# A Conformer convolution module with MLP: the convolution of two spilled blocks in taps of 1024 tokens instead of 512, and three PSUM banks for products instead of five

## The chip, the cores and the metric

One NeuronCore of a Trainium2 chip runs the kernel; all work is float32 in and out. The metric is the device time of one execution in microseconds (us). Before the change it is 1913.57 us, the median of 3 runs (1912.0 to 1917.03).

## What is computed

x has 2048 tokens of 1024 channels. One layer: the Conformer convolution module on the RMS-normed input, added to x, then a squared-ReLU MLP with a hidden width of 4096, added again.

```python
def conformer_conv(x, w_in, b_in, conv_w, conv_b, ln_g, ln_b, w_out, b_out):
    a, g = jnp.split(x @ w_in + b_in, 2, axis=-1)
    h = a * jax.nn.sigmoid(g)                                  # GLU
    h = depthwise_causal_conv(h, conv_w) + conv_b              # 31 taps, each channel by itself
    h = jax.nn.silu(layer_norm(h, ln_g, ln_b))
    return h @ w_out + b_out

x = x + conformer_conv(rms_norm(x, mix_norm), ...)
x = x + square(relu(rms_norm(x, mlp_norm) @ w1)) @ w2
```

## The kernel before

Channels lie on the 128 partitions, tokens along the free axis. The 1024 channels are KD = 8 channel tiles j, the 2048 tokens NB = 4 blocks b of T = 512. Each fp32 operand is kept as two fp32r halves, a rounded one and the rest (`halves`, L92 on ScalarE and L93 on VectorE or GpSimd), and a product takes three matmuls for each 128 rows of its inner dimension (`mm`, matmul at L163): 24 matmuls for an inner dimension of 1024, 12 for the 512 of one hidden group in `mlp_down`.

**First phase** (up to `front.close()`):

- GLU: for each channel tile j and block b, `glu_mm` takes two PSUM banks with `bank()`, pa for the value and pg for the gate, and fills pa, then pg. `glu` empties them. In block 0 the gate is read on VectorE at L328 (times the RMS factor, into `sg`), then the value at L331 (into `ar`), and h is formed at L335. In the other blocks ScalarE reads the gate (sigmoid, L326), and VectorE the value (L335). Blocks 0 and 1 are kept in SBUF, blocks 2 and 3 go to DRAM (`spill`, one tile for each j and block, with a halo of 30 tokens in front).
- `conv`: 31 taps on VectorE. The first (L349) writes an accumulator `cacc` in PSUM, the other 30 (L352) each read the shifted h and the accumulator and write the accumulator; the last writes over h. Blocks 0 and 1 read h, blocks 2 and 3 a tile `hc` of 128x542 that was loaded from `spill`.
- Stats and LayerNorm: `Stats.add` sums the channel tiles (L215), TensorE forms the mean (L226), the variance for each token (L235) and spreads the inverse root (L262), all on one bank of its own (`lps`). For blocks 2 and 3, `ln_spilled` does the taps, the mean, the subtraction (L387), the squares and the last step (`normalised`, L357), and each of its three steps writes `conv_out` in DRAM and loads it again for the next.
- `project` (evicted at L404), its later norm (L412) and split (L93); `mlp_up` and `mlp_down` for eight hidden groups g of 512 channels, `mlp_down` evicted at L440, all for blocks 0 and 1. `mlp_up` ends with two steps on ScalarE (L427 and the square) and the split of hid on VectorE (L93).

**Second phase**: the projection and MLP of blocks 2 and 3 with other pools (L631 and on), which take over the PSUM of the first.

Every accumulator, product and statistic lies in PSUM's 8 banks of 128x512 fp32: in the first phase `lps` takes 1, the pool `psp` of products 5, the pool `psc` of convolution accumulators 2. `bank()` hands out the banks of `psp` as they come free: a product can start when the one that last had its bank has been emptied.

The program is written in the order above; a scheduler merges it into one order for each engine by data, buffers and priority. The taps have no near deadline and fill VectorE's order wherever nothing else is ready. Each engine works its own order strictly in turn; an eviction that stands behind taps waits for them. All loads of the tiles named here go through the DMA queue of SP.

Of the kernel before, what the change touches and what calls it, by code (L numbers as in the profile page):

```python
# [59 lines left out]
def conformer_mlp(ctx: ExitStack, tc, xT, w_in, w_out, w1, w2, vecs, conv_w, outT):  # L60
# [8 lines left out]
    psp = front.enter_context(tc.tile_pool(name="psp", bufs=5, space=PSUM))  # L69
    psc = front.enter_context(tc.tile_pool(name="psc", bufs=2, space=PSUM))  # L70
# [229 lines left out]
    spill = [[dram.tile([P, HALO + T], F32, name=f"spill{j}_{i}") for i in range(2)] for j in range(KD)]  # L300
    conv_out = [[dram.tile([P, T], F32, name=f"conv{j}_{i}") for i in range(2)] for j in range(KD)]
# [20 lines left out]
    def glu(j, b, pa, pg, rs=None):  # L322
# [13 lines left out]
        if b == 0:  # L336
            nc.gpsimd.memset(h[:, :HALO], 0.0)
        else:
            nc.scalar.copy(h[:, :HALO], tails[j])
        if b < NB - 1:  # L340
            nc.scalar.copy(tails[j], h[:, T : T + HALO])
        if not keep:
            nc.sync.dma_start(spill[j][b - 2], h[:, : HALO + T])
# [3 lines left out]
    def conv(j, h):  # L347
        acc = psc.tile([P, T], F32, name="cacc", tag="cacc")
        nc.vector.tensor_scalar(acc, h[:, 0:T], cw[:, j, 0:1], v(V_CB + j), ALU.mult, ALU.add)  # L349
        for k in range(1, TAPS):  # L350
            out = acc if k < TAPS - 1 else h[:, HALO : HALO + T]
            nc.vector.scalar_tensor_tensor(out, h[:, k : k + T], cw[:, j, k : k + 1], acc, ALU.mult, ALU.add)  # L352
        return h[:, HALO : HALO + T]
# [23 lines left out]
    def ln_spilled(i):  # L377

        st = Stats(True)
        for j in range(KD):  # L380
            c = conv(j, stream("hc", spill[j][i], HT, "hc"))
            st.add(j, c)
            nc.sync.dma_start(conv_out[j][i], c)
        mu = st.mean()
        for j in range(KD):
            c = stream("c", conv_out[j][i], tag="hc")
            nc.vector.tensor_sub(c, c, mu)  # L387
            st.add_square(j, c, nc.vector)
            nc.sync.dma_start(conv_out[j][i], c)
        rs = st.rstd()  # L390
        for j in range(KD):
            s = normalised(j, stream("xc", conv_out[j][i], tag="hc"), rs)
            nc.sync.dma_start(conv_out[j][i], s)
# [138 lines left out]
    for i in range(2):  # L532
        ln_spilled(i)
# [175 lines left out]
    def second_input(i):  # L709
        ss = Split()  # L710
        for j in range(KD):
            ss.add(loaded(conv_out[j][i], "s"))
# [349 lines left out]
```

## Time and profile before

| | |
|---|---|
| runs | 1917.03, 1912.0, 1913.57 us; median 1913.57 |
| profiled execution | 1916.64 us, of it a span of 1914.9 us |
| mean granted clock of TensorE | 0.994 |
| busy | TensorE 98%, its weight loads 80%, VectorE 82%, ScalarE 40%, GpSimd 22% |
| taps of blocks 2 and 3 | 16 L349, 464 L352 into `cacc`, 16 L352 into `hc` |
| moved by DMA | 257.96 MB, mean 135 GB/s |

How to read it. Times of the trace are from the start of the span. A timeline row gives start, length, engine, line, operation, output<-inputs, the number of like instructions in sequence, and in brackets the idle time of that engine just before, with what ended it. A group row gives busy time and the mean length of one instruction, then the idle time of the engine before these. Matmuls are pipelined, so the length of one is longer than the distance from one to the next. Line numbers are those of the kernel before; in the changed kernel, lines from L349 on stand 1 lower in `conv` (L350, L353) and 8 lower from `project` on (L412 is L420, L440 is L448).

### The profile page before, as it was taken

The numbers are of one execution on the slowest core, as the hardware profiler recorded it, in microseconds if no ns is written. First come the engines' busy times: TensorE is split into PE (matmuls) and PEld (weight loads), VectorE is DVE, ScalarE is ACT, GpSimd is POOL, SyncE is SP. The second block draws the span as 40 slices with busy tenths as digits, with TensorE's granted clock in tenths as the row PEclk, the third lists the DMA queues.
The fourth block names the chain that finished last, engine by engine and source line by source line (L and its number), as shares of the span: only waits on it lengthen the run. The fifth ranks groups of instructions, "written<-read, shape, count | busy, mean of one in ns | idle before, by whom it ended". The sixth has DMA issues, their size and how long they took to land.

```text
span 1914.9 us, 22348 instructions
## 1 busy us (share of the span) xinstructions
PE 1872.0 (98%) x8192; PEld 1533.9 (80%) x8192; DVE 1576.6 (82%) x2216; ACT 766.1 (40%) x1100; POOL 417.2 (22%) x303
## 2 busy tenths in 40 slices
PE   7999999999989999999999999999999999999999
PEld 5888888888867877877888877778888887888887
DVE  7999999999999999869999974468765648869684
ACT  5323226243353333343323142436544556435431
POOL 2255522544434651000000001122100000010000
PEclk9999999999999999999999999999999999999999
DMA  5123221422223433373212146866534326677652
GB/s 207 66 89 98 98 83 62 143 101 91 97 72 106 148 110 112 113 251 110 89 63 71 66 144 217 266 219 209 203 138 163 123 104 218 180 186 186 143 143 99
DMA packets 114733, 257.96 MB, mean 135 GB/s; under 512 B 10560, under 2 KB 37312, under 8 KB 114624
## 3 DMA queue, kind: packets, MB, share of 16 engines
q1 hardware_dynamic: 104128, 219.84, 34.7%
q0 software_dynamic: 10496, 36.71, 7.4%
q8 instruction: 64, 1.05, 0.2%
q14 instruction: 45, 0.37, 0.1%
HBM read 194.39 MB, written 62.11 MB: 134 GB/s over the span
## 4 chain that ended last, share of the span: by engine, by line
PE 32%; issue 16%; DVE 4%; DMA 4%; POOL 2%; ACT 1%; SPq 0%; POOLq 0%; DVEq 0%; ACTq 0%
PE ps L163 17%; PE px L631 7%; PE pz L631 3%; PE px L163 3%; PE py L631 2%; DVE act L573 1%; POOL hid L746 1%; DMA s<-conv 1%; DVE w L605 1%; DMA conv<-s 1%; DMA rawq<-in_w 1%; DVE ld L866 1%; DMA conv<-c 0%; DMA c<-conv 0%; POOL p L796 0%
## 5 line engine op out<-in xcount | busy, mean ns | idle before, releaser
L163 PE MATMUL ps<-act,w 128*128 128x512 f32 x2880 | 666.1, 391 | 11.6 <-ACT w L92 9.2
L163 PEld LDWEIGHTS ps<-act,w 128*128 128x128 f32 x2880 | 541.3, 188 | 128.2 <-ACT w L92 9.2
L163 PE MATMUL ps<-hid,w 128*128 128x512 f32 x1920 | 445.4, 391 | 6.6 <-DVE hid L93 5.5
L163 PEld LDWEIGHTS ps<-hid,w 128*128 128x128 f32 x1920 | 360.0, 188 | 86.9 <-DVE hid L93 8.0
L631 PE MATMUL px<-act,w 128*128 128x512 f32 x1536 | 363.0, 391 | 3.4 <-DVE act L573 1.4
L631 PEld LDWEIGHTS px<-act,w 128*128 128x128 f32 x1536 | 289.0, 188 | 65.6 <-DVE act L573 2.1
L352 DVE SCALAR_TENSOR_TENSOR cacc<-hc,cw,cacc 128x512 f32<-128x512 f32 x464 | 324.8, 750 | 1.4
L352 DVE SCALAR_TENSOR_TENSOR cacc<-h,cw,cacc 128x512 f32<-128x512 f32 x464 | 317.0, 750 | 0.0
L93 POOL TENSOR_TENSOR w<-raw,w 128x1024 fp32r<-128x1024 f32 x90 | 217.2, 2413 | 287.6 <-ACT w L92 285.1
L92 ACT CAST w<-raw 128x1024 fp32r<-128x1024 f32 (+1 forms) x150 | 155.0, 1035 | 288.1 <-PE ps L163 283.5
L604 ACT CAST w<-rawq 128x1024 fp32r<-128x1024 f32 (+1 forms) x120 | 105.6, 880 | 209.2 <-PE px L631 103.8
L631 PE MATMUL pz<-act,w 128*128 128x512 f32 x768 | 182.5, 389 | 1.3 <-DVE p L729 1.3
L631 PEld LDWEIGHTS pz<-act,w 128*128 128x128 f32 x768 | 143.9, 188 | 32.3 <-ACT w L604 1.2
L605 DVE TENSOR_TENSOR w<-rawq,w 128x1024 fp32r<-128x1024 f32 (+1 forms) x120 | 121.6, 1019 | 45.8 <-ACT w L604 45.7
L440 DVE TENSOR_TENSOR h<-h,ps 128x512 f32<-128x512 f32 x128 | 86.9, 684 | 28.3 <-PE ps L163 26.6
L427 ACT ACTIVATE relu<-ps 128x512 f32<-128x512 f32 x64 | 38.2, 597 | 161.0 <-PE ps L163 160.7
L163 PE MATMUL px<-act,w 128*128 128x512 f32 x384 | 93.5, 404 | 5.2 <-DVE act L93 2.5
L163 PEld LDWEIGHTS px<-act,w 128*128 128x128 f32 x384 | 74.5, 195 | 23.3 <-DVE act L93 3.9
L631 PE MATMUL py<-act,w 128*128 128x512 f32 x384 | 90.9, 389 | 0.0
L631 PEld LDWEIGHTS py<-act,w 128*128 128x128 f32 x384 | 72.1, 188 | 15.0
L93 DVE TENSOR_TENSOR w<-raw,w 128x1024 fp32r<-128x1024 f32 (+1 forms) x60 | 71.0, 1187 | 15.4 <-ACT w L92 15.3
L215 POOL TENSOR_TENSOR acc<-acc,hc 128x512 f32<-128x512 f32 x12 | 14.0, 1165 | 252.1 <-DVE hc L352 202.0
(139 smaller groups left out, 1557.7 us busy)
## 6 DMA issues: line engine op xcount, KB each, us to landing
raw<-in_w SPq DMA_DIRECT2D x104, 512.0 KB, 3.9
rawq<-in_w SPq DMA_DIRECT2D x76, 512.0 KB, 3.9
xt<-in_xT SPq DMA_DIRECT2D x64, 256.0 KB, 3.7
ld<-hid SPq DMA_DIRECT2D x32, 512.0 KB, 5.6
raw<-in_w_in SPq DMA_DIRECT2D x30, 512.0 KB, 3.3
raw<-in_w_out SPq DMA_DIRECT2D x16, 512.0 KB, 3.4
rawq<-in_w_out SPq DMA_DIRECT2D x16, 512.0 KB, 5.8
x<-x SPq DMA_DIRECT2D x32, 256.0 KB, 3.9
```

The lines of the kernel that those rows point to most:

```text
L92: nc.scalar.copy(hl[:, 0, :], src)
L93: eng.tensor_sub(hl[:, 1, :], src, hl[:, 0, :].bitcast(F32))
L163: nc.tensor.matmul(ps, lhsT=w(k, a), rhs=x[:, b, :], start=k == 0 and i == 0, stop=k == len(xs) - 1 and i == 2,)
L352: nc.vector.scalar_tensor_tensor(out, h[:, k : k + T], cw[:, j, k : k + 1], acc, ALU.mult, ALU.add)
L427: nc.scalar.activation(r, ps, AF.Relu)
L440: nc.vector.tensor_add(x2[i][m], x2[i][m], ps)
L573: nc.vector.tensor_sub(t[:, 1], src, t[:, 0].bitcast(F32))
L604: nc.scalar.copy(hl[:, 0, :n], src)
L605: eng.tensor_sub(hl[:, 1, :n], src, hl[:, 0, :n].bitcast(F32))
L631: nc.tensor.matmul(ps, lhsT=hl[:, a, off : off + P], rhs=x[:, b, :], start=first and k == 0 and i == 0, stop=k == n - 1 and i == 2, skip_g ...
L746: nc.gpsimd.dma_start(hid_d[self.q // 4][:, self.q % 4, i : i + t.shape[1], :], t)
L866: nc.vector.tensor_sub(r[t], r[a], r[b])
```

## The change

The convolution of blocks 2 and 3 is done for both at once. `spill[j]` holds both blocks in a row (the halo, block 2, block 3), so block 3 needs no halo copies of its own. `conv_spilled` loads 128x1054 into a new tile `hw`, runs 31 taps of 128x1024 over an accumulator of 1024 fp32 (two banks, one buffer), adds each half to its own `Stats`, and writes both halves with one transfer. Then `ln_spilled` runs for block 2 and for block 3. The 496 taps of 512 become 248 of 1024; 16 loads of spill become 8, and 16 first writes of `conv_out` 8. PSUM: `lps` 1, `cacc512` 2, `cacc1024` 2, so `psp` has 3 banks left.

```diff
-    psp = front.enter_context(tc.tile_pool(name="psp", bufs=5, space=PSUM))
-    psc = front.enter_context(tc.tile_pool(name="psc", bufs=2, space=PSUM))
+    psp = front.enter_context(tc.tile_pool(name="psp", bufs=3, space=PSUM))
+    psc = front.enter_context(tc.tile_pool(name="psc", bufs=1, space=PSUM))
...
-    spill = [[dram.tile([P, HALO + T], F32, name=f"spill{j}_{i}") for i in range(2)] for j in range(KD)]
-    conv_out = [[dram.tile([P, T], F32, name=f"conv{j}_{i}") for i in range(2)] for j in range(KD)]
+    spill = [dram.tile([P, HALO + 2 * T], F32, name=f"spill{j}") for j in range(KD)]
+    conv_out = [dram.tile([P, 2, T], F32, name=f"conv{j}") for j in range(KD)]
...
         if not keep:
-            nc.sync.dma_start(spill[j][b - 2], h[:, : HALO + T])
+            at, end = (0, HALO + T) if b == 2 else (HALO + T, HALO + 2 * T)
+            nc.sync.dma_start(spill[j][:, at:end], h[:, HALO + T - (end - at) : HALO + T])
...
-    def conv(j, h):
-        acc = psc.tile([P, T], F32, name="cacc", tag="cacc")
+    def conv(j, h, n=T):
+        acc = psc.tile([P, n], F32, name="cacc", tag=f"cacc{n}", bufs=2 if n == T else 1)
...
-            out = acc if k < TAPS - 1 else h[:, HALO : HALO + T]
-            nc.vector.scalar_tensor_tensor(out, h[:, k : k + T], cw[:, j, k : k + 1], acc, ALU.mult, ALU.add)
+            out = acc if k < TAPS - 1 else h[:, HALO : HALO + n]
+            nc.vector.scalar_tensor_tensor(out, h[:, k : k + n], cw[:, j, k : k + 1], acc, ALU.mult, ALU.add)
...
-    def ln_spilled(i):
-
-        st = Stats(True)
+    def conv_spilled():
+
+        sts = [Stats(True) for _ in range(2)]
         for j in range(KD):
-            c = conv(j, stream("hc", spill[j][i], HT, "hc"))
-            st.add(j, c)
-            nc.sync.dma_start(conv_out[j][i], c)
+            h = sb.tile([P, HALO + 2 * T], F32, name="hw", tag="hw", bufs=2)
+            nc.sync.dma_start(h, spill[j])
+            c = conv(j, h, 2 * T)
+            for i in range(2):
+                sts[i].add(j, c[:, i * T : (i + 1) * T])
+            nc.sync.dma_start(conv_out[j], c.rearrange("p (i c) -> p i c", i=2))
+        return sts
+
+    def ln_spilled(i, st):
+
         mu = st.mean()
...
-    for i in range(2):
-        ln_spilled(i)
+    for i, st in enumerate(conv_spilled()):
+        ln_spilled(i, st)
     front.close()
```

What the scheduler makes of it, at three places.

TensorE, the pair of products of channel tile 0 of block 1 (`ps_551` is its value and `ps_552` its gate before; `ps_535` and `ps_536` after; the matmuls of a `glu_mm` pair may be mixed by the scheduler). Before:

```order
L163 MATMUL ps_426<-act_181,hid_330 128x512 x3
L163 MATMUL ps_551<-act_483,w_130 128x512 x3
L163 MATMUL ps_551<-act_491,w_130 128x512 x3
L163 MATMUL ps_551<-act_499,w_130 128x512 x3
L163 MATMUL ps_551<-act_507,w_130 128x512
L163 MATMUL ps_552<-act_483,w_131 128x512 x3
L163 MATMUL ps_551<-act_507,w_130 128x512 x2
```

and now:

```order
L163 MATMUL ps_410<-act_165,hid_314 128x512 x3
L163 MATMUL ps_535<-act_467,w_114 128x512 x3
L163 MATMUL ps_535<-act_475,w_114 128x512 x3
L163 MATMUL ps_535<-act_483,w_114 128x512 x3
L163 MATMUL ps_535<-act_491,w_114 128x512 x3
L163 MATMUL ps_535<-act_499,w_114 128x512 x3
L163 MATMUL ps_535<-act_507,w_114 128x512 x3
L163 MATMUL ps_535<-act_515,w_114 128x512
L163 MATMUL ps_536<-act_467,w_115 128x512 x3
```

The gate's first three matmuls stood behind 10 of the value's; now they stand behind 19.

VectorE, the first two channel tiles of block 0 (L328 reads the gate, the two rows here of product 1's bank and of product 3's; `cacc` are taps of channel tile 0). Before:

```order
L328 TENSOR_TENSOR sg<-ps,rstd 128x512
L215 TENSOR_TENSOR acc<-acc,sq 128x512
L331 TENSOR_TENSOR ar<-ps,rstd 128x512
L215 TENSOR_TENSOR acc<-acc,sq 128x512
L335 SCALAR_TENSOR_TENSOR h<-ar,vec,sg 128x512
L349 TENSOR_SCALAR cacc<-h,cw,vec 128x512
L352 SCALAR_TENSOR_TENSOR cacc<-h,cw,cacc 128x512
L328 TENSOR_TENSOR sg<-ps,rstd 128x512
L331 TENSOR_TENSOR ar<-ps,rstd 128x512
```

and now:

```order
L328 TENSOR_TENSOR sg<-ps,rstd 128x512
L215 TENSOR_TENSOR acc<-acc,sq 128x512
L331 TENSOR_TENSOR ar<-ps,rstd 128x512
L215 TENSOR_TENSOR acc<-acc,sq 128x512
L335 SCALAR_TENSOR_TENSOR h<-ar,vec,sg 128x512
L350 TENSOR_SCALAR cacc<-h,cw,vec 128x512
L353 SCALAR_TENSOR_TENSOR cacc<-h,cw,cacc 128x512 x3
L328 TENSOR_TENSOR sg<-ps,rstd 128x512
L331 TENSOR_TENSOR ar<-ps,rstd 128x512
```

Two more taps stand ahead of the second gate's eviction, and so ahead of all that follows it.

TensorE, the statistics of the spilled blocks. Before, those of block 3 stood in the last pair of hidden groups before the second phase (its first product is `px`), and block 2's L226 stood 1349 matmuls of products ahead of block 3's:

```order
L163 MATMUL ps<-act,w 128x512 x100
L226 MATMUL lps<-acc,inv 128x512
L163 MATMUL ps<-act,w 128x512 x77
L235 MATMUL lps<-inv,acc 128x1 x4
L163 MATMUL ps<-act,w 128x512 x10
L262 MATMUL lps<-dg,inv_r 128x512
L163 MATMUL ps<-act,w 128x512 x2
L262 MATMUL lps<-dg,inv_r 128x512
L163 MATMUL ps<-act,w 128x512 x3
L163 MATMUL ps<-hid,w 128x512 x192
L163 MATMUL px<-act,w 128x512 x216
```

and now they stand 94 matmuls of products apart (446 more follow the last row shown before `px`):

```order
L163 MATMUL ps<-act,w 128x512 x80
L226 MATMUL lps<-acc,inv 128x512
L163 MATMUL ps<-act,w 128x512 x80
L235 MATMUL lps<-inv,acc 128x1 x4
L163 MATMUL ps<-act,w 128x512 x8
L262 MATMUL lps<-dg,inv_r 128x512
L163 MATMUL ps<-act,w 128x512 x2
L262 MATMUL lps<-dg,inv_r 128x512
L163 MATMUL ps<-act,w 128x512 x4
L226 MATMUL lps<-acc,inv 128x512
L163 MATMUL ps<-act,w 128x512 x18
L163 MATMUL ps<-hid,w 128x512 x130
```

Counted from `px`, block 2's L226 stood 1633 matmuls ahead and now stands 688 ahead; block 3's stood 284 ahead and now 594.

## Rows read from the trace of the kernel before

**Rows 1.** the page, part 1: busy time, share of the span, instructions of each engine

```profile
PE 1872.0 (98%) x8192; PEld 1533.9 (80%) x8192; DVE 1576.6 (82%) x2216; ACT 766.1 (40%) x1100; POOL 417.2 (22%) x303
```

**Rows 2.** two stretches: engines' busy time (instructions), granted clock, DMA share, GB/s

```profile
500.00:1150.00 650.00, 634.61 (x2775) 518.64 (x2774) 592.81 (x860) 236.55 (x335) 125.78 (x66) 0.99 0.34 112
...
800.00:850.00 50.00, 48.17 (x206) 38.58 (x205) 35.31 (x57) 22.31 (x33) 2.11 (x2) 0.97 0.62 201
```

**Rows 3.** groups of VectorE, whole span: busy, mean ns, idle before

```profile
L352 DVE SCALAR_TENSOR_TENSOR cacc<-hc,cw,cacc 128x512 f32<-128x512 f32 x464 | 324.8, 750 | 1.4
...
L573 DVE TENSOR_TENSOR act<-ld,act 128x1024 fp32r<-128x1024 f32 x48 | 57.2, 1219 | 9.0 <-ACT act L572 9.0
...
L93 DVE TENSOR_TENSOR act<-n,act 128x512 fp32r<-128x512 f32 x20 | 13.2, 682 | 0.0
```

**Rows 4.** timeline of VectorE near 703 us: start, length, line, count

```profile
703.48 4.70 DVE L352 SCALAR_TENSOR_TENSOR cacc<-hc,cw,cacc 128x512 f32<-128x512 f32 x7
```

**Rows 5.** timeline of TensorE, 20 to 206 us, first phase

```profile
27.23 10.16 PE L163 MATMUL ps<-act,hid 128*128 128x512 f32 x44
...
49.51 11.55 PE L163 MATMUL ps<-act,w 128*128 128x512 f32 x48
...
106.52 70.23 PE L163 MATMUL ps<-act,w 128*128 128x512 f32 x309
...
194.89 11.04 PE L163 MATMUL ps<-hid,w 128*128 128x512 f32 x48
```

**Rows 6.** timelines of VectorE and ScalarE: the gates' evictions in that stretch

```profile
30.54 0.69 DVE L328 TENSOR_TENSOR sg<-ps,rstd 128x512 f32<-128x512 f32 x1
...
55.18 0.69 DVE L328 TENSOR_TENSOR sg<-ps,rstd 128x512 f32<-128x512 f32 x1
...
123.65 0.68 DVE L328 TENSOR_TENSOR sg<-ps,rstd 128x512 f32<-128x512 f32 x1
...
201.28 0.68 ACT L326 ACTIVATE sg<-ps,vec 128x512 f32<-128x512 f32 x1
```

**Rows 7.** timeline of VectorE: two waits for TensorE's statistics

```profile
99.96 0.16 DVE L244 TENSOR_SCALAR var<-lps 128x4 f32<-128x4 f32 x1 [0.85 <-PE lps L235]
...
677.54 0.16 DVE L244 TENSOR_SCALAR var<-lps 128x4 f32<-128x4 f32 x1 [0.78 <-PE lps L235]
```

**Rows 8.** timeline of TensorE around 690 us, between two MLPs

```profile
684.10 10.39 PE L163 MATMUL ps<-hid,w 128*128 128x512 f32 x45
...
694.33 3.80 PE L163 MATMUL ps<-act,w 128*128 128x512 f32 x16
...
702.42 9.82 PE L163 MATMUL ps<-act,w 128*128 128x512 f32 x42 [1.81 <-DVE act L93]
```

**Rows 9.** timeline of VectorE there: two evictions of mlp_down

```profile
693.85 0.67 DVE L440 TENSOR_TENSOR h<-h,ps 128x512 f32<-128x512 f32 x1
...
699.50 0.68 DVE L440 TENSOR_TENSOR h<-h,ps 128x512 f32<-128x512 f32 x1
```

**Rows 10.** groups of TensorE, 500 to 1150 us: idle before, by releaser

```profile
L163 PE MATMUL ps<-act,w 128*128 128x512 f32 x1536 | 355.5, 392 | 2.4 <-DVE act L93 2.4
...
L163 PE MATMUL ps<-hid,w 128*128 128x512 f32 x1193 | 277.3, 392 | 5.4 <-DVE hid L93 4.3 <-ACT hid L92 1.1
```

**Rows 11.** timeline of TensorE: its waits at both LayerNorms of spilled blocks

```profile
833.64 1.05 PE L235 MATMUL lps<-inv,acc 128*128 128x1 f32 x8 [1.50 <-DVE acc L215]
...
862.99 7.37 PE L163 MATMUL ps<-hid,w 128*128 128x512 f32 x31 [1.11 <-ACT hid L92]
...
1141.34 1.05 PE L235 MATMUL lps<-inv,acc 128*128 128x1 f32 x8 [0.66 <-DVE acc L215]
...
1145.40 0.47 PE L262 MATMUL lps<-dg,inv_r 128*128 128x512 f32 x1 [0.61 <-DVE dg L255]
```

**Rows 12.** groups of VectorE, 800 to 865 us: LayerNorm of block 2

```profile
L357 DVE TENSOR_TENSOR y<-xc,rstd 128x512 f32<-128x512 f32 x8 | 5.4, 690 | 4.6 <-ACT rstd L265 2.2 <-DMA conv<-s 1.9 <-ACT s L359 0.5
...
L387 DVE TENSOR_TENSOR c<-c,mean 128x512 f32<-128x512 f32 x8 | 5.4, 689 | 5.9 <-issue 3.1 <-DMA c<-conv 2.7
```

More of the change, by code (lines that the diff above doesn't have):

```diff
@@ L337, in glu @@
             nc.gpsimd.memset(h[:, :HALO], 0.0)
-        else:
+        elif b < 3:
             nc.scalar.copy(h[:, :HALO], tails[j])
-        if b < NB - 1:
+        if b < 2:
             nc.scalar.copy(tails[j], h[:, T : T + HALO])
         if not keep:
-            nc.sync.dma_start(spill[j][b - 2], h[:, : HALO + T])
-        return h
-    def conv(j, h):
-        acc = psc.tile([P, T], F32, name="cacc", tag="cacc")
-        nc.vector.tensor_scalar(acc, h[:, 0:T], cw[:, j, 0:1], v(V_CB + j), ALU.mult, ALU.add)
+            at, end = (0, HALO + T) if b == 2 else (HALO + T, HALO + 2 * T)
+            nc.sync.dma_start(spill[j][:, at:end], h[:, HALO + T - (end - at) : HALO + T])
+        return h
+    def conv(j, h, n=T):
+        acc = psc.tile([P, n], F32, name="cacc", tag=f"cacc{n}", bufs=2 if n == T else 1)
+        nc.vector.tensor_scalar(acc, h[:, 0:n], cw[:, j, 0:1], v(V_CB + j), ALU.mult, ALU.add)
         for k in range(1, TAPS):
-            out = acc if k < TAPS - 1 else h[:, HALO : HALO + T]
-            nc.vector.scalar_tensor_tensor(out, h[:, k : k + T], cw[:, j, k : k + 1], acc, ALU.mult, ALU.add)
-        return h[:, HALO : HALO + T]
+            out = acc if k < TAPS - 1 else h[:, HALO : HALO + n]
+            nc.vector.scalar_tensor_tensor(out, h[:, k : k + n], cw[:, j, k : k + 1], acc, ALU.mult, ALU.add)
+        return h[:, HALO : HALO + n]
     def normalised(j, xc, rs):
@@ L375, in ln_kept @@
         return [act_split(normalised(j, hs[j][:, HALO : HALO + T], rs)) for j in range(KD)]
-    def ln_spilled(i):
-        st = Stats(True)
+    def conv_spilled():
+        sts = [Stats(True) for _ in range(2)]
         for j in range(KD):
-            c = conv(j, stream("hc", spill[j][i], HT, "hc"))
-            st.add(j, c)
-            nc.sync.dma_start(conv_out[j][i], c)
+            h = sb.tile([P, HALO + 2 * T], F32, name="hw", tag="hw", bufs=2)
[6 more added lines that the diff above has]
+    def ln_spilled(i, st):
         mu = st.mean()
         for j in range(KD):
-            c = stream("c", conv_out[j][i], tag="hc")
+            c = stream("c", conv_out[j][:, i, :], tag="hc")
             nc.vector.tensor_sub(c, c, mu)
             st.add_square(j, c, nc.vector)
-            nc.sync.dma_start(conv_out[j][i], c)
+            nc.sync.dma_start(conv_out[j][:, i, :], c)
         rs = st.rstd()
         for j in range(KD):
-            s = normalised(j, stream("xc", conv_out[j][i], tag="hc"), rs)
-            nc.sync.dma_start(conv_out[j][i], s)
+            s = normalised(j, stream("xc", conv_out[j][:, i, :], tag="hc"), rs)
+            nc.sync.dma_start(conv_out[j][:, i, :], s)
     def project(b, ss, eng=nc.vector):
@@ L711, in second_input @@
         for j in range(KD):
-            ss.add(loaded(conv_out[j][i], "s"))
+            ss.add(loaded(conv_out[j][:, i, :], "s"))
         return ss.parts()
```

## The prediction

> **What bounds the kernel now.** I read the shares of the engines first: TensorE is busy 1872.0 of 1914.9 us, 98%, VectorE 82% [rows 1]. Whatever the change does to VectorE, it can shorten the kernel only where TensorE stands idle, and lengthens it wherever TensorE has to wait anew. Then the stretch in which the taps of blocks 2 and 3 lie, 500 to 1150 us: TensorE is busy 634.61 of 650 us there, so 15.4 us are idle, with VectorE busy 592.81, 91% [rows 2]. That 15.4 us is all that a lighter VectorE could give back directly. Next the groups of TensorE by releaser in that stretch: 2.4 us before products of act and 5.4 before products of hid, all behind VectorE or ScalarE and none behind an occupied bank [rows 10]. The rest is at the LayerNorms [rows 11]. Last I laid the timelines of TensorE and of the engine that empties the banks side by side [rows 5, 6, 8, 9], because the change leaves three banks of five. Five banks hide late evictions, so no wait of before shows what three would cost; it must be worked out from when each bank was emptied.
>
> The sum is made against the profiled execution, 1916.64 us, which stands 3.1 above the median of 1913.57.
>
> **The taps.** A row of seven taps takes 4.70 us, one alone 0.75 [rows 3, 4], so the distance between taps is (4.70 − 0.75) / 6 = 0.658 us. No row shows a tap of 1024. The nearest are VectorE's splits: 1219 ns for 1024, 682 for 512 [rows 3], so 512 more tokens cost 0.537 us. A tap of 1024 should then be 1.29 us long and stand 0.658 + 0.537 = 1.195 us from the next, where two of 512 took 1.316. Per pair that saves 0.121 us, and 248 × 0.121 = 30 us of VectorE. The bounds are nothing saved (the second bank costs as much as a second tap), and 0.213 a pair (what lies between 0.75 and 0.537), 53 us. I take 30, since both splits are the same operation at the two widths. None of it is on the path by itself: TensorE's 98% covers it, and without that cover it would be worth up to the 30.
>
> That VectorE's relief reaches TensorE is the point where a rule has to be weighed. The rows say that TensorE lost 15.4 us in 650 while VectorE was 91% busy [rows 2], and that the waits hang on a chain (sum, mean, square, split), less on how many taps there are. The Trainium skill, Perfetto Trace Analysis, section Optimizing Scalar/DVE Operations, says that grouping into larger operations can improve throughput if the engine is saturated. By that rule the sum would be up to −15.4, by the rows about nothing from this term. I count nothing here and keep the −15.4 as a rival.
>
> DMAs: 8 loads of spill and 8 writes of conv_out fewer on SP's queue, the same bytes, and no wait of TensorE in the groups on any of them [rows 10]. The fewer halo copies are short work on ScalarE, 40% busy [rows 1]. Both cost nothing; without their cover they would be a gain too small to see.
>
> **Three banks in the GLU.** I count products from 0; 0 and 1 are value and gate of channel tile 0 in block 0. A pair takes two of three banks. The next value takes the third, and the next gate must take the bank that comes free first, which is that of the gate before it. So gate n waits until gate n−2 has been emptied, with only one value product, 24 matmuls, in between. Of the 32 pairs, four break this by the times of before:
>
> - Product 3 starts 11 matmuls into the row at 27.23: 27.23 + 11 × 10.16/44 = 29.77. Gate 1 is emptied at 30.54 + 0.69 = 31.23 [rows 5, 6]. Wait 1.46.
> - Product 7: in the new order its first matmul stands behind 19 of product 6's: 49.51 + 19 × 11.55/48 = 54.08, and 55.5 with the delay so far. Gate 5 is emptied at 55.18 + 0.69, and two more taps now stand ahead of it on VectorE, + 1.32: 57.2 [rows 5, 6]. Wait 1.7.
> - Product 19 starts 69 matmuls into the row at 106.52: 106.52 + 69 × 70.23/309 = 122.20. Gate 17 is emptied at 123.65 + 0.68, less 0.66 because 13 taps now stand where 14 stood after VectorE's last wait for TensorE: 123.67 [rows 5, 6]. Wait 1.5.
> - Product 33, half into the row at 194.89: 200.41. ScalarE empties gate 31 at 201.28 + 0.68 = 201.96 [rows 5, 6]. Wait 1.55.
>
> They add up instead of covering each other, because VectorE itself waits for TensorE between them, 0.85 us at 99.96 and 0.78 at 677.54 [rows 7], and so slides back with it. Sum 6.2 us.
>
> **Three banks between the MLPs.** Around 690 us the evictions of mlp_down (group 4, block 0) stand on VectorE behind eight normalisations and splits. Product n here waits for the eviction of product n−3. Product 139, the last of mlp_down, starts 33 matmuls into the row at 684.10: 684.10 + 33 × 10.39/45 = 691.72; the bank is free at 693.85 + 0.67 = 694.52 [rows 8, 9], wait 2.8. Product 140 would start at 694.33 + 2.8 = 697.13; its bank is free at 699.50 + 0.68 = 700.18 [rows 8, 9], wait 3.05. Together 5.85, less the 2.4 that the same products already waited for their splits there [rows 10], of which 1.81 at 702.42 [rows 8]: net 3.5. VectorE's order has the same evictions behind the same normalisations, so I see nothing that brings them forward.
>
> A stretch in which TensorE waited also showed a lower granted clock: 0.97 over 800 to 850 us [rows 2], full speed (2.4 GHz) for most of it and the lower level (1.2 GHz) for some; that is 0.03 × 50 = 1.5 us. I count one such dip near 690: + 1.5.
>
> **Longer steps before a hand-off.** Splits of hid that TensorE waits for stand behind a tap. The four waits of this kind (5.4 us [rows 10]) grow by half of the 1.195 − 0.658 = 0.54 us: 4 × 0.27 = + 1.1.
>
> **The LayerNorms.** Block 2's moves from 806 to 863 us back to block 3's. Its waits of 1.50 and 1.11 us [rows 11] and the dip of 1.5 [rows 2] go: − 4.1. Beside block 3's it should cost what that one costs now, 0.66 + 0.61 = 1.27 [rows 11]. Net − 2.8. Its bounds: − 4.1 if it hides wholly, and the last rival if it doesn't.
>
> Sum: 6.2 + 3.5 + 1.5 + 1.1 − 2.8 = **+ 9.5 us**; on the median 1913.6 + 9.5 = 1923.1, so 1923.
>
> **The rivals.**
>
> *Faster: VectorE's relief reaches TensorE.* If the evictions come earlier throughout, because 30 us of taps are gone, no bank waits and the 15.4 us of idle time go: 1913.6 − 15.4 = 1898. It decides at the four gates above: they must be emptied 1.5 us earlier. For it speaks VectorE's 91% [rows 2]; against it that those gates lie ahead of 205 us, where taps of 512 are done in both kernels, and that the relief comes later. By the skill's rule on grouping this is the case; the chance is mine, 0.12.
>
> *No change: the bank waits don't come.* VectorE's slack moves, the scheduler's taps fall elsewhere, and only the LayerNorm and the hand-offs are left: 1.1 − 2.8 = − 1.7, 1912. For it speaks that most pairs have over 2 us to spare, against it that each wait follows from an eviction's own row. Chance 0.22.
>
> *Much slower: two LayerNorms back to back.* In block 2's pass VectorE stood 5.9 + 4.6 = 10.5 us before its subtractions and last steps, for the transfers through conv_out and for ScalarE [rows 12]. Five banks covered most of that. With three, an mlp_down product of 12 matmuls may run one product, 12 × 0.227 = 2.7 us (the spacing of product 19's row [rows 5]), into such a gap. If both passes stand one behind the other, 2 × (10.5 − 2.7) = 15.6 more: 1939. Against it: taps left over from VectorE's filling can't be there any more, since all taps come first, which frees VectorE for evictions. Chance 0.11.
>
> *The change doesn't do what it says* would be a tap of 1024 as dear as two of 512; that is the bound above. The taps then end 30 us later than I count, still ahead of the second phase, and the time stays at 1923.
>
> **How the numbers follow.** Chances: forecast 0.55, no change 0.22, faster 0.12, much slower 0.11. About 0.3%, 5.7 us, is what a measurement of this kernel can tell from no change. The forecast's own range is 1917 to 1930: single waits of some 1.5 us can fail or be joined by another (gate 21 had 0.2 us to spare by the same reckoning, with more taps ahead of it now, some 2.5). The range is 1906 to 1941: it takes in no change and its lower side, and the much slower case; the faster case mostly stays out. Faster 0.13, within the bound 0.23, slower 0.64.
>
> **What would show it.** Right: waits of TensorE before products of ps behind VectorE's or ScalarE's gate evictions near 31, 57, 124 and 202 us, of 1 to 3 us each, and two behind L448 near 695 us, 5 to 6 together; taps of 128x1024 with a mean of 1.25 to 1.33 us; the last tap some 30 us earlier than before; no LayerNorm of block 2 near 830. Wrong: no such wait (no change or faster), idle time of TensorE in the last two hidden groups over 5 us (much slower), or a mean tap of 1.45 us and more.

## The result, and the profile after

| | before | after |
|---|---|---|
| runs (us) | 1917.03, 1912.0, 1913.57, 1916.25 | 1934.67, 1937.71, 1938.2, 1940.83 |
| median (us) | 1914.91 | 1937.95 |
| granted clock of TensorE in those of after | | 0.991, 0.989, 0.988, 0.986 |
| profiled execution's span (us) | 1914.9 | 1932.9 |

The change makes the kernel slower: ratio 1.0115, 95% interval 1.0099 to 1.0131, some 22 us (23 by the medians). The forecast was slower by 9.5, with 1923; the direction came, and the forecast's size is less than half of it. 1937.95 lies in the range of 1906 to 1941 and outside the forecast's own 1917 to 1930.

Page of the changed kernel, part 1, to be read against [rows 1]:

```profile
PE 1881.5 (97%) x8192; PEld 1540.0 (80%) x8192; DVE 1553.2 (80%) x1968; ACT 762.2 (39%) x1082; POOL 419.0 (22%) x303
```

This line holds much of the answer. TensorE does the same 8192 instructions and is busy 1881.5 instead of 1872.0 us: 9.5 us more for the same work. Its idle time is 1932.9 − 1881.5 = 51.4 us where it was 1914.9 − 1872.0 = 42.9: 8.5 more. So of the 18 us between the two spans nearly one half is waiting, and the rest is matmuls that took longer. Some 7 us of that rest go with a lower granted clock, as the windows show; what the other 2.5 are is not shown by any run.

Where the clock was lower is seen in windows. Columns: stretch, its length, TensorE's busy time (instructions), granted clock, DMA share, GB/s. Before:

```profile
290.00:312.00 22.00, 21.71 (x100) 1.00 0.11 36
565.00:585.00 20.00, 20.00 (x90) 1.00 0.33 104
700.00:722.00 22.00, 20.19 (x89) 1.00 0.38 121
...
545.00:600.00 55.00, 50.78 (x219) 0.97 0.26 83
...
1030.00:1160.00 130.00, 128.73 (x568) 1.00 0.35 114
```

and after:

```profile
290.00:312.00 22.00, 19.17 (x75) 0.84 0.13 49
565.00:585.00 20.00, 16.52 (x63) 0.83 0.17 52
700.00:722.00 22.00, 18.13 (x72) 0.92 0.18 56
...
545.00:600.00 55.00, 50.26 (x208) 0.94 0.28 92
...
1030.00:1160.00 130.00, 125.08 (x544) 0.99 0.53 178
```

A clock of 0.84 as a mean is full speed (2.4 GHz) for most of the stretch and the lower level (1.2 GHz) for the rest: (1 − 0.84) × 22 = 3.5 us are lost, in the second stretch 0.17 × 20 = 3.4, in the third 0.08 × 22 = 1.8. Before, a like dip stood at 550, ahead of the second stretch. The stretch of 545 to 600 us holds both: 0.03 × 55 = 1.65 us lost before, 0.06 × 55 = 3.3 after, so 1.65 of it is a net loss. The dip of 800 to 850 us before [rows 2], 1.5 us, is made up for by one of 0.01 × 130 = 1.3 in the last stretch. Together 3.5 + 1.65 + 1.8 − 0.2, some 7 us. The mean clocks of the two spans, 0.994 and 0.991, give 17.4 − 11.5 = 5.9 us, where their rounding leaves some 1 us open on each side.

The four gates of the GLU and the two products near 706 us, from the timeline of TensorE after the change (these answer to [rows 5, 8]):

```profile
31.80 7.73 PE L163 MATMUL ps<-act,hid 128*128 128x512 f32 x33 [1.47 <-DVE sg L328]
...
53.85 2.12 PE L163 MATMUL ps<-act,w 128*128 128x512 f32 x8 [0.77 <-DVE act L93]
...
126.57 54.70 PE L163 MATMUL ps<-act,w 128*128 128x512 f32 x240 [1.41 <-DVE sg L328]
...
205.49 5.75 PE L163 MATMUL ps<-hid,w 128*128 128x512 f32 x24 [1.00 <-ACT sg L326]
...
706.41 4.61 PE L163 MATMUL ps<-hid,w 128*128 128x512 f32 x12 [2.74 <-DVE h L448]
...
712.16 22.05 PE L163 MATMUL ps<-act,w 128*128 128x512 f32 x96 [1.13 <-ACT w L92]
```

The reader is to see waits at four of the products that were named (3, 19, 33, 139). The three gate waits name the gate's eviction, L328 or L326, and the one at 706 names L448. Product 7 shows none of its own. The 0.77, and the 0.40 before the next row at 56.37, stand before the 11th and the 19th matmul of product 6 and are put down to splits of act. Product 7's first matmul is the 20th of the pair, so it lies inside the row at 56.37, and gate 5, whose bank it takes, is emptied on VectorE by 56.93:

```profile
56.24 0.69 DVE L328 TENSOR_TENSOR sg<-ps,rstd 128x512 f32<-128x512 f32 x1
```

The orders of both kernels suggest how these two waits come from the missing banks all the same: before, the gate's first matmuls stood behind the value's 10th; now the value's 11th stands there and has to wait for its split. At 706 us, 12 matmuls take 4.61 us instead of 2.7.

And one wait that nothing had announced, at the LayerNorm of block 0. TensorE before:

```profile
283.75 10.13 PE L163 MATMUL ps<-hid,w 128*128 128x512 f32 x42
293.72 2.65 PE L163 MATMUL ps<-act,w 128*128 128x512 f32 x11
296.66 1.02 PE L235 MATMUL lps<-inv,acc 128*128 128x1 f32 x8 [0.29 <-DVE acc L215]
297.55 3.43 PE L163 MATMUL ps<-act,w 128*128 128x512 f32 x14
```

and after:

```profile
288.39 6.05 PE L163 MATMUL ps<-hid,w 128*128 128x512 f32 x26
297.27 1.36 PE L235 MATMUL lps<-inv,acc 128*128 128x1 f32 x8 [2.83 <-DVE acc L215]
298.50 5.89 PE L163 MATMUL ps<-hid,w 128*128 128x512 f32 x13
```

The wait is 2.83 us instead of 0.29, and the 13 matmuls behind it take 5.89 us, 0.45 each, where before 14 took 3.43, 0.245 each. VectorE is hardly later (the wait ends at 297.27 and ended at 296.66). It is the order that moved: block 0's L226 and L235 now stand 33 matmuls earlier among the products, as the scheduler's order for TensorE shows. Before:

```
L163 MATMUL ps<-hid,w 128x512 x6
L226 MATMUL lps<-acc,inv 128x512
L163 MATMUL ps<-hid,w 128x512 x42
L163 MATMUL ps<-act,w 128x512 x11
L235 MATMUL lps<-inv,acc 128x1 x4
```

and after, where 27 + 26 = 53 matmuls stand between the two as 42 + 11 did, and the pair as a whole has moved ahead (in the product row ahead, 21 of 48 are done at L226, where all 48 and 6 of the next were):

```
L163 MATMUL ps<-act,w 128x512 x21
L226 MATMUL lps<-acc,inv 128x512
L163 MATMUL ps<-act,w 128x512 x27
L163 MATMUL ps<-hid,w 128x512 x26
L235 MATMUL lps<-inv,acc 128x1 x4
```

33 matmuls are 7.5 us of TensorE, while the chip had made TensorE only 5.2 later by then. The remainder is the wait. That the scheduler assumed a later TensorE is inferred from this shift; the runs show only the shift and the wait.

To see what each stretch contributes I compared the start of every 24th matmul of L163 in the two traces (a product of `mlp_down` has 12, so from the first `mlp_down` on these steps have lower numbers than the products of the prediction); the delay of the profiled execution after against before grows like this:

| up to step of 24 matmuls (time before) | delay | what lies there |
|---|---|---|
| 33 (200 us) | 5.2 | the four gates |
| 49 (288) | 5.6 | |
| 52 (307) | 11.2 | LayerNorm of block 0 |
| 98 (572) | 10.9 | LayerNorm of block 1: as before |
| 121 (703) | 14.7 | mlp_down and the normalisation |
| 140 (810) | 13.4 | |
| 149 (865) | 7.3 | LayerNorm of block 2 no longer here |
| 200 (1147) | 15.6 | both LayerNorms of the spilled blocks |
| end | 17.9 | second phase |

Lastly the taps, from the groups of VectorE after the change, answering to [rows 3]:

```profile
L353 DVE SCALAR_TENSOR_TENSOR cacc<-hw,cw,cacc 128x1024 f32<-128x1024 f32 x232 | 298.0, 1285 | 3.8
...
L350 DVE TENSOR_SCALAR cacc<-hw,cw,vec 128x1024 f32<-128x1024 f32 x8 | 10.7, 1342 | 5.1 <-DMA hw<-spill 5.0
```

1285 ns is the 1.29 us that was worked out from the splits. The distance from tap to tap is not the 1.195 that was worked out. Three in a row after:

```profile
821.64 3.93 DVE L353 SCALAR_TENSOR_TENSOR cacc<-hw,cw,cacc 128x1024 f32<-128x1024 f32 x3
```

They stand (3.93 − 1.28)/2 = 1.32 us apart, as much as two of 512 (1.316 [rows 4]). The groups agree: 464 × 750 ns = 348 us of taps took 324.8 before, because each overlaps the next a little; 232 × 1285 ns = 298.1 took 298.0, with no overlap. The trace of before shows where the overlap comes from. Two accumulators are in use there, and the taps of two channel tiles alternate (first two rows); where the last tile is alone, its taps stand (4.71 − 0.75)/5 = 0.79 us apart instead of 0.658 (third row):

```profile
508.19 0.75 DVE L352 SCALAR_TENSOR_TENSOR cacc<-h,cw,cacc 128x512 f32<-128x512 f32 x1
508.85 0.75 DVE L352 SCALAR_TENSOR_TENSOR cacc<-hc,cw,cacc 128x512 f32<-128x512 f32 x1
...
1101.90 4.71 DVE L352 SCALAR_TENSOR_TENSOR cacc<-hc,cw,cacc 128x512 f32<-128x512 f32 x6
```

The accumulator of 1024 is the only one of its kind, so each tap waits for the one whose result it reads. VectorE's busy time as a whole fell by 1576.6 − 1553.2 = 23.4 us.

### The profile page after: what moved, and what is told of

It is laid out like the page before. It is cut to its first block, busy times and chain, and to the rows that moved or that the text cites. A ratio compares the mean times of both kernels' runs of the same rounds, so it can differ in the third digit from the quotient of the medians.

```text
span 1932.9 us, 22031 instructions
## 1 busy us (share of the span) xinstructions
PE 1881.5 (97%) x8192; PEld 1540.0 (80%) x8192; DVE 1553.2 (80%) x1968; ACT 762.2 (39%) x1082; POOL 419.0 (22%) x303
## 5 line engine op out<-in xcount | busy, mean ns | idle before, releaser
L163 PE MATMUL ps<-act,w 128*128 128x512 f32 x2880 | 667.8, 392 | 12.2 <-ACT w L92 9.5
L163 PEld LDWEIGHTS ps<-act,w 128*128 128x128 f32 x2880 | 543.5, 189 | 129.7 <-ACT w L92 8.4
L163 PE MATMUL ps<-hid,w 128*128 128x512 f32 x1920 | 451.2, 394 | 10.1 <-DVE hid L93 6.4
L163 PEld LDWEIGHTS ps<-hid,w 128*128 128x128 f32 x1920 | 362.8, 190 | 92.1 <-DVE hid L93 9.0
L353 DVE SCALAR_TENSOR_TENSOR cacc<-hw,cw,cacc 128x1024 f32<-128x1024 f32 x232 | 298.0, 1285 | 3.8
L93 POOL TENSOR_TENSOR w<-raw,w 128x1024 fp32r<-128x1024 f32 x90 | 221.1, 2456 | 305.1 <-ACT w L92 300.0
L448 DVE TENSOR_TENSOR h<-h,ps 128x512 f32<-128x512 f32 x128 | 86.7, 681 | 38.1 <-PE ps L163 37.3
L163 PE MATMUL px<-act,w 128*128 128x512 f32 x384 | 93.8, 405 | 5.4 <-DVE act L93 2.7
L163 PEld LDWEIGHTS px<-act,w 128*128 128x128 f32 x384 | 74.5, 195 | 23.9 <-DVE act L93 4.3
L215 POOL TENSOR_TENSOR acc<-acc,hw 128x512 f32<-128x512 f32 x12 | 14.2, 1206 | 283.4 <-issue 237.1
```

The costliest lines, as they stand in the source:

```text
L93: eng.tensor_sub(hl[:, 1, :], src, hl[:, 0, :].bitcast(F32))
L163: nc.tensor.matmul(ps, lhsT=w(k, a), rhs=x[:, b, :], start=k == 0 and i == 0, stop=k == len(xs) - 1 and i == 2,)
L215: eng.tensor_add(self.acc, self.acc, t)
L353: nc.vector.scalar_tensor_tensor(out, h[:, k : k + n], cw[:, j, k : k + 1], acc, ALU.mult, ALU.add)
L448: nc.vector.tensor_add(x2[i][m], x2[i][m], ps)
```

## The experiments

**Which half of the change costs.** The first run gives the change its five banks back: one accumulator of two banks serves both widths, so that the taps of blocks 0 and 1 too have one accumulator where they had two.

```diff
-    psp = ... name="psp", bufs=3
+    psp = ... name="psp", bufs=5
-        acc = psc.tile([P, n], F32, name="cacc", tag=f"cacc{n}", bufs=2 if n == T else 1)
+        acc = psc.tile([P, 2 * T], F32, name="cacc", tag="cacc")[:, :n]
```

> The change with five banks for products: one accumulator of two banks serves the taps of 512 and of 1024. Bank theory (the loss comes from three banks: the waits behind the gates at 31, 57, 126 and 205 us and behind mlp_down near 706 us, and the slower clock behind them): 1912 to 1920, no wait of a product behind L328, L326 or L448 in the first phase. LayerNorm theory (the loss comes from both LayerNorms standing one behind the other at 1040 to 1150 us, where TensorE fell back by 8.3 us): 1922 to 1930, with waits before L235 near 1050 and 1095 us of over 1 us each.

Measured: 1928.92 us against 1915.57, ratio 1.0071 (1.0045 to 1.0097). No product waits behind L328, L326 or L448 in the first phase, but the statistics do, and at 1154 a product waits 2.75 us for a split of hid. So with five banks some 13 us of the loss stay, and the bank theory doesn't cover them. But this run changes VectorE's work as well. Its page, and a row of its taps of 512:

```profile
PE 1875.0 (97%) x8192; PEld 1533.8 (80%) x8192; DVE 1581.1 (82%) x1968; ACT 764.6 (40%) x1084; POOL 423.4 (22%) x303
...
61.26 10.25 DVE L353 SCALAR_TENSOR_TENSOR cacc<-h,cw,cacc 128x512 f32<-128x512 f32 x13
```

With one accumulator the taps of blocks 0 and 1 stand (10.25 − 0.75)/12 = 0.79 us apart instead of 0.658, and VectorE is busier (1581.1 us) than in the kernel before. How much of the 13 us that costs is not shown; the third run keeps two accumulators.

The second run takes two banks from the kernel before, and nothing else.

```diff
-    psp = ... name="psp", bufs=5
+    psp = ... name="psp", bufs=3
```

> The kernel before with three banks for products instead of five, taps of 512, nothing else. Bank theory: 1926 to 1934, with the four gate waits (1.4 to 1.8 us each) and about 5 us lost at 690 us. LayerNorm theory: 1920 to 1924, the gate waits alone.

Measured: 1943.42, ratio 1.0144 (1.0112 to 1.0176): 28 us, above both forecasts and no less than the whole change (the intervals overlap). The waits behind L328, L326 and the eviction of `mlp_down` come at the same products as in the change, with longer ones elsewhere, such as 2.65 us at 602.6 for a split of hid (1.26 at 600.0 in the change). Two rows of TensorE, at the LayerNorm of block 0 and at that of block 2, which here still has its old place:

```profile
298.04 1.18 PE L235 MATMUL lps<-inv,acc 128*128 128x1 f32 x8 [2.79 <-DVE acc L215]
...
837.53 10.74 PE L163 MATMUL ps<-hid,w 128*128 128x512 f32 x39 [2.54 <-ACT hid L92]
```

The wait of 2.8 us at block 0's LayerNorm is thus a matter of three banks, not of the taps. At block 2's, where five banks left waits of 1.50 and 1.11 us [rows 11], three leave one of 2.54 before a product, and 39 matmuls in 10.74 us behind it.

The third run has the order of the change (both blocks in one loop, LayerNorms back to back), with taps of 512 and five banks.

```diff
-            c = conv(j, h, 2 * T)
-            for i in range(2):
-                sts[i].add(j, c[:, i * T : (i + 1) * T])
+            c = h[:, HALO : HALO + 2 * T]
+            for i in (1, 0):
+                sts[i].add(j, conv(j, h[:, i * T : i * T + HT]))
```

> The order of the change (both spilled blocks tap by tap in one loop, their LayerNorms back to back) with taps of 512 and five banks. Bank theory: 1911 to 1919. LayerNorm theory: 1922 to 1930. Against the run with five banks and taps of 1024 it shows what the wider tap is worth: 30 us of VectorE, 0 to 5 us of time.

Measured: 1924.68, ratio 1.0050 (1.0032 to 1.0068), 9 us. TensorE runs within 2 us of the kernel before down to 810 us, gains 6 where block 2's LayerNorm no longer stands, and then:

```profile
1102.87 1.05 PE L235 MATMUL lps<-inv,acc 128*128 128x1 f32 x8 [1.59 <-DVE acc L215]
...
1146.99 1.86 PE L235 MATMUL lps<-inv,acc 128*128 128x1 f32 x8 [4.79 <-DVE acc L215]
1148.72 2.48 PE L163 MATMUL ps<-act,w 128*128 128x512 f32 x5
```

The second block's statistics wait 4.79 us for VectorE, and the five matmuls behind them take 2.48, twice their time. Moving block 2's LayerNorm next to block 3's is no gain even with five banks. Against the first run (1928.92, the same with taps of 1024) the wider tap shows no gain, but that comparison isn't clean, because the first run's taps of blocks 0 and 1 are dearer; the intervals overlap, so a loss isn't shown either. Both theories keep a part, and the parts don't add: 28 for the banks alone and 9 for the order alone, 23 for all. With five banks the order costs 9; with three (1943.42 against 1937.95) order and wide taps together show no cost; a gain of some 5 is possible, but these intervals overlap too, and its cause isn't shown.

**What the relief of VectorE is worth.** The kernel before, with three taps of each tile of blocks 2 and 3 left out:

```diff
-        for k in range(1, TAPS):
+        for k in range(1 + skip, TAPS):
...
-            c = conv(j, stream("hc", spill[j][i], HT, "hc"))
+            c = conv(j, stream("hc", spill[j][i], HT, "hc"), 3)
```

> The kernel before with three taps of each channel tile of blocks 2 and 3 left out (taps 1 to 3, so 48 x 0.658 = 31.6 us of VectorE work less; the output is not the reference's), five banks, taps of 512. It gives the relief that the wider taps were to give, and nothing else. Cover theory (VectorE's taps lie beside TensorE's work): 1910 to 1918. Relief theory (less tap work brings evictions and statistics forward): 1898 to 1906.

Measured: 1916.47 against 1913.99, ratio 1.0010 (0.9998 to 1.0023). The page of this run:

```profile
PE 1869.7 (98%) x8192; PEld 1532.0 (80%) x8192; DVE 1545.1 (81%) x2168; ACT 767.1 (40%) x1100; POOL 416.1 (22%) x303
```

VectorE is busy 1545.1 us instead of 1576.6, and 32 us less work on it bring nothing that can be measured. This was the whole point of the wider tap, and it fails without any cost on the other side.

**How many banks.** As the first run, with four:

```diff
-    psp = ... name="psp", bufs=5
+    psp = ... name="psp", bufs=4
```

> The change with four banks for products (the accumulator of two banks is shared by both widths of tap). If a gate waits only because three banks serve two products at a time, four banks are as good as five: no wait behind a gate's eviction, 1925 to 1932. If every bank counts, between the run with five and the change: 1931 to 1936.

Measured: 1932.62, ratio 1.0095 (1.0074 to 1.0116), between five (1928.92) and three (1937.95), with intervals that overlap. Only the run with five has the same single accumulator, so only that comparison is of the banks alone. No gate wait, as forecast. Whether the fifth bank matters elsewhere is not settled by it.

**Is a wait paid twice?** Ahead of L235 in the LayerNorms of blocks 0 and 1, extra matmuls on the same bank, which L235 overwrites; they can start when the last square is there. First six, in the changed kernel and in the one before (there in block 1 alone), then three.

```diff
             pv = self.bank()
+            for _ in range(self.fill):
+                nc.tensor.matmul(pv, lhsT=inv, rhs=self.last, start=True, stop=True)
```

> The changed kernel with six extra matmuls of 128x512 (their result is overwritten) ahead of L235 in the LayerNorms of blocks 0 and 1, where TensorE waited 2.83 us at 297 and 3.48 us at 571 and then showed 12 matmuls each at 0.45 us instead of 0.227. Clock theory (a wait of that length is paid twice, the second time by a slow stretch behind it): the waits shrink or go, the slow matmuls behind them go, 4 to 7 us less than the change, 1931 to 1934. Wait theory (only the idle time counts): 0 to 1 us, 1937 to 1939, since the extra matmuls only take the place of the idle time.

> The kernel before with the same six extra matmuls in the LayerNorm of block 1 alone (a wait of 3.03 us at 550 and 7 slow matmuls behind it). Clock theory: 1 to 3 us faster than before, 1911 to 1914. Wait theory: no change, 1914 to 1916.

Measured: 1937.57 (ratio 1.0115, 1.0091 to 1.0138) and 1924.44 (1.0044, 1.0027 to 1.0061). No gain, and a loss of some 8 to 10 us for the kernel before. The filling was the wrong size: in the run on the changed kernel it took 5.42 us, and TensorE waited 1.52 for it all the same:

```profile
294.45 5.42 PE L236 MATMUL lps<-sq,inv 128*128 128x512 f32 x12 [1.52 <-ACT sq L219]
```

With three:

> As the run with six extra matmuls in the LayerNorms of blocks 0 and 1 of the change, with three: they took 0.9 us each there, 5.4 us in all, where a wait of 2.83 or 3.48 us was to be filled; three take 2.7. Clock theory: no slow matmuls at 298 and 572 us, TensorE 2 to 3 us earlier than the change behind each of the two, 1931 to 1935. Wait theory: no gain, 1936 to 1940.

> The kernel before with three extra matmuls in the LayerNorm of block 1, where it waits 3.03 us at 550 and shows 7 slow matmuls. Clock theory: 1 to 3 us earlier behind it, 1911 to 1914, hardly to be told from before by the total; the cumulated delay by product tells. Wait theory: no gain or a loss of up to 2.7.

Measured: 1939.75 (1.0122, 1.0091 to 1.0152) and 1917.24 (1.0014, 0.9999 to 1.0029). By the total both miss the clock theory. At the place itself the slow matmuls go. The changed kernel with three, TensorE's timeline at the LayerNorms of blocks 0 and 1:

```profile
294.12 2.84 PE L236 MATMUL lps<-sq,inv 128*128 128x512 f32 x6 [1.55 <-ACT sq L219]
296.79 1.01 PE L238 MATMUL lps<-inv,acc 128*128 128x1 f32 x8
297.67 3.46 PE L163 MATMUL ps<-hid,w 128*128 128x512 f32 x14
...
561.16 2.84 PE L236 MATMUL lps<-sq,inv 128*128 128x512 f32 x6 [3.37 <-ACT sq L219]
...
564.65 4.39 PE L163 MATMUL ps<-hid,w 128*128 128x512 f32 x18
```

and the window of the first:

```profile
290.00:312.00 22.00, 19.88 (x85) 1.00 0.14 49
```

14 matmuls in 3.46 us where 13 took 5.89, granted clock 1.00 where it was 0.84, and behind the place TensorE is 1.5 us ahead of the change; 0.5 of that it had before, and 2 to 3 had been expected. At block 1 the slow matmuls go too (18 in 4.39 us, where 21 took 7.44 in the change), although the wait ahead of the extra matmuls is as long as the wait in the change, 3.37 against 3.48 us, and TensorE gains nothing. In the kernel before, 14 matmuls take 3.48 us instead of 5.04, but a new wait of 1.99 us at 553 leaves TensorE later than without the filling. So the slow stretch doesn't hang on the length of the wait alone; with matmuls between the wait and L235 it doesn't come. And the gain isn't kept: the order shifts, and the changed kernel with three is 2.3 us behind the change by 700 us and 5 at the end. That a wait can be paid twice is shown at these places; that mending one place lowers the time is not.

**Repairs for three banks.** The gate's product first, which doubles the time that a gate's eviction has:

```diff
-        pa, pg = bank(), bank()
-        mm(pa, w[0], xs)
-        mm(pg, w[1], xs)
+        pg, pa = bank(), bank()
+        mm(pg, w[1], xs)
+        mm(pa, w[0], xs)
```

> The changed kernel (three banks) with the gate's product ahead of the value's in each GLU pair, so that the next pair's second product, not one product earlier, needs the bank of the gate that came out first. Bank theory: the four waits behind gates at 32, 58, 127 and 205 us (1.47, 1.17, 1.41 and 1.00 us) go, TensorE is 4 to 6 us earlier at 280 us than in the change, and the time is 1930 to 1934. If VectorE or ScalarE is simply late, the waits stay under other names: 1936 to 1940.

Measured: 1935.43, ratio 1.0098 (1.0073 to 1.0122). Product 33's wait is gone; near 126 us:

```profile
124.96 6.19 PE L163 MATMUL ps<-act,w 128*128 128x512 f32 x26 [0.70 <-DVE sg L328]
...
132.07 3.26 PE L163 MATMUL ps<-act,w 128*128 128x512 f32 x13 [0.92 <-POOL h L337]
```

One wait of 1.41 has become two, of 0.70 and 0.92. The second is put down to GpSimd; why it comes isn't shown. TensorE was 1.5 us ahead of the change at 205 us, where 4 to 6 had been expected.

mlp_down's evictions with a high priority:

```diff
-                nc.vector.tensor_add(x2[i][m], x2[i][m], ps)
+                with tc.high_priority():
+                    nc.vector.tensor_add(x2[i][m], x2[i][m], ps)
```

> The changed kernel (three banks) with a high priority for the evictions of mlp_down (L448), so that VectorE's order has them between the normalisations of block 1 instead of behind eight of them. Bank theory with the clock: the wait of 2.74 us at 706 us, the 1.13 behind it and its 9 slow matmuls go, TensorE is 3 to 6 us earlier behind 720 us than in the change, 1931 to 1936. If the splits of act are pushed back by as much, the wait only changes its name: 1936 to 1941.

Measured: 1936.9, ratio 1.0119 (1.0093 to 1.0145). The wait of 2.74 before the last product of mlp_down is gone, and the same engine makes the next products wait instead:

```profile
713.23 0.49 PE L163 MATMUL ps<-act,w 128*128 128x512 f32 x1 [1.71 <-ACT act L92]
715.10 3.35 PE L163 MATMUL ps<-act,w 128*128 128x512 f32 x7 [1.38 <-DVE act L93]
```

The wait changed its name, as the rival had it: VectorE has a chain of evictions, normalisations and splits there that TensorE needs all of.

Both together:

> Three banks with both repairs: the gate's product first, and mlp_down's evictions with a high priority. If the two add up: the sum of what each gained over the change, 1928 to 1934, near the run with five banks (1928.92), since only the statistics' waits and both LayerNorms are left. If the time that is won is lost again at the next statistics: 1934 to 1938.

Measured: 1936.39, ratio 1.0117 (1.0085 to 1.0149). In its trace TensorE is 5.1 us ahead of the change at 718 us and 0.3 at 1157: the time that is won is lost again by the end of the late LayerNorms. Neither repair, nor both, can be told from the change. No version was found that beats the kernel before.

## Why the prediction was right in direction and too small

- **Taps: length right, distance wrong.** 1.29 us was worked out, 1285 ns came. But 1.195 from tap to tap was read from [rows 4], where two accumulators alternate, and one accumulator gives 1.32 in a row: there a tap of 1024 is as dear as two of 512, the bound that the prediction gave; its sign for that, a mean tap of 1.45 us, looked at the length alone. Where another operation follows a tap, it starts earlier (831.27, the next at 832.46). The groups of blocks 2 and 3 sum to 298.0 + 10.7 and 10.2 for the last taps, 318.9 us, against 324.8 + 12.9 + 11.9 = 349.6, 30.7 us less; but these sums count overlaps with other rows twice, and VectorE as a whole is busy 23.4 us less, not 30. The last of these taps ended at 1036.7 us instead of 1120.8, 84 us earlier and not some 30, as all of them now stand ahead of both LayerNorms.
- **Relief worth nothing: right**, by the run with 28 taps. The rule of the Trainium skill (Perfetto Trace Analysis, Optimizing Scalar/DVE Operations) on grouping in a saturated engine would have given up to − 15.4 here by the prediction's working. No run bore it out: VectorE was busy 91% of that stretch [rows 2] and ended most of TensorE's waits there, but with 31.5 us less work on it the time didn't fall.
- **Gates: right** at products 3, 19 and 33. Forecast 1.46, 1.5 and 1.55; measured 1.47, 1.41 and 1.00. At product 7, 1.7 behind the gate was forecast; the 1.17 us there are waits of product 6 for its splits. The sum, 5.1 us against 6.2, is close, in part for another reason than the one given.
- **Between the MLPs: near in time (3.5 and 1.5 for the clock forecast, 3.8 more delay measured), wrong in kind.** Product 139 waited 2.74 for L448 (2.8). Product 140 waited 1.13 instead of 3.05, so the net idle time was 2.74 + 1.13 − 2.4 = 1.5 instead of 3.5. But product 139 itself took 4.61 us instead of 2.7, slow matmuls, and 1.13 + 1.9 is the 3.05 again: product 140, at 712.16, could not start before its bank was free, and TensorE spent that time partly idle and partly slow. The trace puts the 1.13 down to ScalarE, but the eviction that frees the bank ends at 712.01:

```profile
711.34 0.67 DVE L448 TENSOR_TENSOR h<-h,ps 128x512 f32<-128x512 f32 x1
```

- **Hand-offs: near in size.** Waits for splits of hid on VectorE grew from 5.5 to 6.4 us. That says little for the mechanism: one of them, 1.49 us, stands at the late LayerNorms, and the forecast also let block 2's 1.11 us grow here while it took it away there.
- **LayerNorms of the spilled blocks: wrong.** − 2.8 was forecast. Between steps 140 and 200 the delay grew by 2.2. Leaving the old place gave 6.1 us, more than the 4.1 counted, but the new place cost 8.3 instead of 1.27. TensorE's idle time from 1030 to 1160 us grew from 1.3 to 4.9 us (130 − 128.73 and 130 − 125.08), and the clock took 1.3 more. TensorE's timeline there, after:

```profile
1058.64 1.05 PE L235 MATMUL lps<-inv,acc 128*128 128x1 f32 x8 [1.41 <-DVE acc L215]
...
1075.97 24.82 PE L163 MATMUL ps<-hid,w 128*128 128x512 f32 x108 [1.49 <-DVE hid L93]
1102.04 1.05 PE L235 MATMUL lps<-inv,acc 128*128 128x1 f32 x8 [1.26 <-DVE acc L215]
1102.95 4.12 PE L163 MATMUL ps<-hid,w 128*128 128x512 f32 x10
```

  I had priced block 2's pass by what block 3's cost, 0.66 + 0.61 [rows 11], though block 2's own rows stood beside it. At the new place it cost even more than the 6.1 us that it had cost at the old.
- **LayerNorm of block 0: not in the sum.** 2.83 us of waiting and the slow matmuls behind it, 5.7 us of delay. I compared the banks' times with the order of before, and looked for order changes at the gates and at the spilled blocks only.
- **The step that failed is the clock**: "I count one such dip near 690: + 1.5", set off by the dip of 1.5 that block 2's LayerNorm took with it, so zero in the sum. The dip near 690 came, with 1.8 us at 707. But block 0's LayerNorm brought one of 3.5, block 1's grew by 1.65, and block 2's didn't go, it moved along to 1103 us: some 7 us net where the sum had none. TensorE's busy time for the same work grew by 9.5 us, and what the other 2.5 are stays open. The idle terms of the sum are 6.2 + 3.5 + 1.1 − 1.3 = 9.5 us, and 8.5 were measured. That these agree is partly luck: block 0's 2.83 us weren't in the sum, and they fill what is missing at other places. So the waiting was sized about right as a total, and its second price was left out. The kernel before showed it already, at block 1's LayerNorm, where 14 matmuls behind a wait of 3.03 us took 5.04 us; the row after the bracket had to be read too:

```profile
550.06 1.05 PE L235 MATMUL lps<-inv,acc 128*128 128x1 f32 x8 [3.03 <-DVE acc L215]
550.97 5.04 PE L163 MATMUL ps<-hid,w 128*128 128x512 f32 x14
```

- **Much slower** was given as 1939 and the time came out at 1937.95, but not by its mechanism. The 10.5 us a pass by which VectorE would hold TensorE aren't there in full: 15.6 were given for the two, the stretch cost 8.3, with 4.9 us of idle time where the sign was over 5, and the other 10 of the 17.9 lie elsewhere.

The median stands 3.3 us above the profiled execution: the four runs after have granted clocks of 0.991, 0.989, 0.988 and 0.986, in the order of their times, 1934.67 to 1940.83.

What stays open: how much of the loss at the two late LayerNorms and of the last 2.3 us in the second phase is waiting proper and how much follows from where the scheduler put things; every run that changed one thing also shifted the order elsewhere.

## What to carry to other kernels

Where one engine is 98% busy, buffers in front of it are worth more than work taken off its neighbour: 32 us less on VectorE gained nothing here, and two banks fewer, with nothing else changed, cost 28 us. When a change adds waits to TensorE, look in the rows for two prices, the idle time and the matmuls that follow it: behind each of the four waits of 2.7 us and more in the first phase of the kernels before and after (the start apart), some of them ran at half speed here. When a distance between two instructions is read from a trace, look whether they belong to one chain or to two that alternate: with one accumulator the overlap is gone. In a kernel that a scheduler orders, look for statistics and reductions that have moved against the products, not only for what the change names.

## What the runs showed of the hardware that was not expected

- A wait of TensorE is not always followed by a slow stretch, and its length alone doesn't tell. Behind 1.47, 1.41 and 1.00 us (at 31.8, 126.6 and 205.5) the matmuls ran on at 0.23 us; behind 2.83 and 2.74 us some ten ran at 0.45, twice that, full speed being 2.4 GHz and the lower level 1.2. In the run with order alone it was 4.79 us, with slow matmuls behind. But ahead of L235 shorter waits were followed by slow matmuls too: 1.50 us at 833.6 in the kernel before [rows 11] (13 matmuls in 4.82 us), 1.26 at 1102.0 in the changed one (10 in 4.12), and 1.09 in the run with five banks and taps of 1024:

```profile
309.32 1.05 PE L235 MATMUL lps<-inv,acc 128*128 128x1 f32 x8 [1.09 <-DVE acc L215]
310.24 5.04 PE L163 MATMUL ps<-hid,w 128*128 128x512 f32 x14
```

  Yet behind 1.41 at 1058.6, ahead of L235 as well, 8 took 2.11 us, at full speed. What decides is open.
- Taps that alternate between two accumulators stand 0.658 us apart, taps on one accumulator 0.79, both 0.75 us long and of 128x512; of 128x1024 on one accumulator they stand 1.32 apart and are 1.285 long.
- Six fp32 matmuls of 128x512 (12 records) took 5.42 us, 0.90 each, against 0.227 for one of fp32r.
- The changed program's runs differ by 6 us (1934.67 to 1940.83), in the order of their granted clocks. It isn't always so: of the kernel before with three extra matmuls, the run with the highest clock, 0.998, took 1919.73 us and one with 0.996 took 1914.96.
